# Two weights, then two stores: the order of transfers in one software queue of a batched matmul

## The chip, the cores and the metric

One core of a Trainium2 chip runs the kernel; the other cores are idle. PE is its tensor engine, DVE the vector engine, ACT the scalar engine; POOL and SP here mainly issue transfers, which 16 DMA engines carry out; PSUM is the memory that PE writes to. The metric is the device time of one execution in microseconds (us), as a median over repeated runs. A profile is one execution with the hardware profiler; its span runs from the first to the last instruction and is about 1.8 us shorter than the device time of the same run.

## The reference

```python
batch, m, k, n = 32, 512, 1024, 768
x      = randn(batch, m, k)   # float32
weight = randn(batch, k, n)   # float32
out    = matmul(x, weight)    # float32, batch by batch
```

It reads 67.1 MB of x and 100.7 MB of weights and writes 50.3 MB.

## The kernel before

Loads are issued from POOL, whose software queue casts float32 to bf16 on the way. Two batches of x come in one transfer (2 MiB at the destination), each weight in one (1.5 MiB at the destination, 3 MiB read), each output in one (1.5 MiB). PE transposes x through PSUM, then multiplies; ACT and DVE evict the result to `out_sb`. Four weight buffers, three of x, seven of the output. This is the loop's head, where the queue's order is made:

```python
AHEAD, LATE, HELD = 3, 4, 3
...
for b in range(B):                       # B = 32
    if b % 2 and b + AHEAD + 1 < B:
        ...                              # load the pair of x for batches b+4, b+5
    if b + AHEAD < B:
        load_w(b + AHEAD)                # waits until PE has used its buffer
    if b <= B - LATE:
        if b > 0:
            pending.append(b - 1)
        if b + AHEAD < B - HELD or b == B - LATE:
            for at in pending:
                nc.gpsimd.dma_start(out=out_view[at], in_=outs[at])
            pending = []
    ...                                  # transposes, matmuls, evictions of batch b
```

The last four weights are cut into two or three loads, and the last stores go through the SP queue.

## Time and profile before

| | before |
|---|---|
| median of the first 3 runs | 517.4 us (517.32 to 517.96) |
| span of the profiled run | 514.2 us |
| DMA busy | every slice of the span |
| PE busy | 85% |
| PE waits for a weight | 28.8 us in 10 waits |

The page splits the span into 40 slices and gives each engine's busy share in tenths. "DMA" is the mean of 16 DMA engines that work side by side on every transfer. A timeline line has start, duration, engine, source line, operation, tiles, and in brackets the idle time before it with what ended it. The lines themselves are in the prediction below.

### The profile page before, as it was taken

The page shows a single profiled execution, that of the slowest core. Times are in us where ns is not written, and L with a number is a line of the kernel's source. Part 1 is how long each engine was busy: PE and PEld are TensorE (multiplying, and loading weights), DVE is VectorE, ACT ScalarE, POOL GpSimd, SP SyncE. Part 2 cuts the span into 40 slices and gives each one's busy share as a digit, 9 for nine tenths or more (in the row PEclk, how much of TensorE's full clock was granted, in tenths as well). Part 3 has the DMA queues.
Part 4 walks back from the last instruction along what each step waited for, and adds up shares of the span by engine and source line. Part 5 has one row for each costly group of instructions (what it writes and reads, how often), then busy time and mean ns, then how long its engine had stood idle before and what let it go on. Part 6 is the DMA issues. An engine that isn't in the chain of part 4 may idle for free.

```text
span 514.2 us, 5846 instructions
## 1 busy us (share of the span) xinstructions
PE 438.1 (85%) x2576; PEld 279.6 (54%) x2576; DVE 130.0 (25%) x196; ACT 76.1 (15%) x129; POOL 43.8 (9%) x87
## 2 busy tenths in 40 slices
PE   2808999999999797998979889798897979999992
PEld 1506566666666463664636546365564645666561
DVE  1205142323223141231413205032050510514121
ACT  0100111111121111111111111011111111110211
POOL 3000100101010100101001000100001001011000
PEclk9957999999999898898989989799898997999997
DMA  8999999999999999999999999999999999999997
GB/s 240 224 220 214 221 265 289 214 278 273 272 287 213 282 270 276 279 215 293 263 277 275 221 292 250 278 278 224 305 239 277 277 235 306 224 276 214 270 428 318
DMA packets 12904, 135.63 MB, mean 264 GB/s; under 512 B 1488, under 2 KB 1488, under 8 KB 3280
## 3 DMA queue, kind: packets, MB, share of 16 engines
q0 software_dynamic: 11664, 126.88, 96.5%
q1 hardware_dynamic: 1216, 8.39, 4.1%
q8 instruction: 20, 0.33, 0.2%
q14 instruction: 4, 0.03, 0.0%
HBM read 167.77 MB, written 50.33 MB: 424 GB/s over the span
## 4 chain that ended last, share of the span: by engine, by line
PE 61%; DMA 25%; DVE 6%; another core or an unknown queue 4%; issue 1%; SPq 1%; ACT 0%
PE pm L121 54%; DMA w_sb<-in_weight_dram 18%; DMA out_sb<-in_x_dram 7%; PE pt L76 6%; DVE xT L83 4%; DVE out_sb L133 2%; SPq L143 1%; PE pt L103 0%; DVE xT L91 0%; ACT out_sb L134 0%; SPq L140 0%
## 5 line engine op out<-in xcount | busy, mean ns | idle before, releaser
L121 PE MATMUL pm<-w_sb,xT 128*128 128x256 bf16 (+1 forms) x2048 | 356.5, 338 | 28.8 <-DMA w_sb<-in_weight_dram 28.8
L121 PEld LDWEIGHTS <-xT 128*128 128x128 bf16 x2048 | 206.3, 101 | 174.6 <-DMA w_sb<-in_weight_dram 32.1
L133 DVE COPY out_sb<-pm 128x512 f32<-128x512 f32 x64 | 44.2, 691 | 331.8 <-PE pm L121 314.5
L76 PE MATMUL pt<-ident,x_sb 128*128 128x128 f32 x496 | 79.8, 302 | 10.5 <-DVE xT L83 10.2
L76 PEld LDWEIGHTS pt<-ident,x_sb 128*128 128x128 f32 x496 | 69.2, 209 | 21.5 <-DVE xT L83 18.7
L83 DVE COPY xT<-pt 128x1024 bf16<-128x1024 bf16 x120 | 77.4, 687 | 11.0 <-PE pt L76 11.0
L132 ACT COPY out_sb<-pm 128x512 f32<-128x512 f32 x64 | 37.4, 585 | 283.6 <-PE pm L121 276.0
L134 ACT COPY out_sb<-pm 128x512 f32<-128x512 f32 x64 | 37.5, 585 | 144.1 <-PE pm L121 144.0
L68 POOL DMA_DIRECT2D w_sb<-in_weight_dram x37 | 19.7, 533 | 328.7 <-PE pm L121 298.9
L167 POOL DMA_DIRECT2D out_dram<-out_sb x28 | 15.0, 536 | 60.3 <-DMA w_sb<-in_weight_dram 22.7
L103 PE MATMUL pt<-ident,out_sb 128*128 128x128 f32 x8 | 1.9, 421 | 16.2 <-DMA out_sb<-in_x_dram 16.2
L103 PE MATMUL pt<-ident,x_sb 128*128 128x128 f32 x24 | 5.2, 377 | 10.4 <-DMA x_sb<-in_x_dram 10.3
L104 DVE CAST xT<-pt 128x512 bf16<-128x512 f32 x8 | 5.9, 734 | 31.4 <-PE pt L103 31.1
L58 POOL DMA_DIRECT2D x_sb<-in_x_dram x15 | 8.0, 533 | 33.4 <-DMA out_dram<-out_sb 22.6
L103 PEld LDWEIGHTS pt<-ident,out_sb 128*128 128x128 f32 x8 | 1.6, 218 | 16.5 <-issue 16.5
L103 PEld LDWEIGHTS pt<-ident,x_sb 128*128 128x128 f32 x24 | 4.1, 210 | 11.3 <-issue 10.2
L91 DVE COPY xT<-pt 128x1024 bf16<-128x1024 bf16 x4 | 2.6, 686 | 0.2 <-PE pt L76 0.2
L132 ACT ACT_TABLE_LOAD x1 | 1.3, 1283 | 0.7 <-PEq L221 0.7
L62 POOL DMA_DIRECT2D x_sb<-in_x_dram x1 | 0.5, 527 | 6.7 <-DMA w_sb<-in_weight_dram 6.7
masks.py:199 POOL TENSOR_SCALAR_AFFINE_SELECT ident<-ident 128x128 f32<-128x128 f32 x1 | 0.3, 287 | 0.1
masks.py:197 POOL MEMSET ident<- 128x128 f32 x1 | 0.2, 223 | 0.0
L221 POOL MEMSET const-float32-0.0<- 128x1 f32 x1 | 0.1, 98 | 0.2 <-issue 0.2
(3 smaller groups left out, 0.3 us busy)
## 6 DMA issues: line engine op xcount, KB each, us to landing
w_sb<-in_weight_dram POOLq DMA_DIRECT2D x28, 1536.0 KB, 45.5
out_dram<-out_sb POOLq DMA_DIRECT2D x28, 1536.0 KB, 45.8
x_sb<-in_x_dram POOLq DMA_DIRECT2D x15, 2048.0 KB, 52.1
w_sb<-in_weight_dram POOLq DMA_DIRECT2D x7, 768.0 KB, 38.3
out_dram<-out_sb SPq DMA_DIRECT2D x4, 768.0 KB
out_dram<-out_sb SPq DMA_DIRECT2D x2, 1536.0 KB
x_sb<-in_x_dram SPq DMA_DIRECT2D x1, 1536.0 KB
x_sb<-in_x_dram POOLq DMA_DIRECT2D x1, 1024.0 KB, 36.2
```

The source lines that it names most:

```text
L58: nc.gpsimd.dma_start(out=xs[b], in_=pair_view[b // 2])
L68: nc.gpsimd.dma_start(out=ws[b][:, at:at + n, :], in_=w_view[b, :, at:at + n, :])
L76: nc.tensor.transpose(pt[:, j, :], pairs[:, mo, j::JT], ident)
L83: nc.vector.tensor_copy(both[:, :, :, :, half, :].rearrange("p b j i r -> p j b i r"), words(b, mt + MT * half).rearrange("p j (b i r) -> ...
L103: nc.tensor.transpose(pt[:, i, :], rows[:, JT * h + i::KT], ident)
L104: nc.vector.tensor_copy(xT[:, 2 * h:2 * h + 2].rearrange("p j m r -> p j r m"), pt.rearrange("p (j r) m -> p j r m", r=2),)
L121: nc.tensor.matmul(pm[bank][:, at:at + size], xT[:, ko // 2, :, ko % 2], ws[b][:, ko, off:off + size], start=(ko == 0 and not (together an ...
L132: nc.scalar.copy(o[:, 0:512], pm[0])
L133: nc.vector.tensor_copy(o[:, 512:1024], pm[1])
L134: nc.scalar.copy(o[:, 1024:N2], pm[2])
L143: nc.sync.dma_start(x_fourth[rows, 0], x_view[0, rows, MT - 1])
L167: nc.gpsimd.dma_start(out=out_view[at], in_=outs[at])
```

## The change

Its intent is to let loads follow loads and stores follow stores: in place of weight, store, weight, store, each pair of batches puts weight, weight, store, store into the software queue.

```diff
@@ -162,7 +162,7 @@
             if b <= B - LATE:
                 if b > 0:
                     pending.append(b - 1)
-                if b + AHEAD < B - HELD or b == B - LATE:
+                if b % 2 == 0 and b + AHEAD < B - HELD or b == B - LATE:
                     for at in pending:
                         nc.gpsimd.dma_start(out=out_view[at], in_=outs[at])
                     pending = []
```

A side effect at the end: the store of batch 24 moves behind the last weight.

## The prediction

> **What bounds the kernel now.** I read the page first for which engine is full, then the busy time by stage, then the waits of the tensor engine, then the issues of the software queue (POOL) in order of time, and last the end of the kernel.
>
> From the page (slices, queues, traffic):
>
> ```profile
> DMA  8999999999999999999999999999999999999997
> ...
> q0 software_dynamic: 11664, 126.88, 96.5%
> q1 hardware_dynamic: 1216, 8.39, 4.1%
> ...
> HBM read 167.77 MB, written 50.33 MB: 424 GB/s over the span
> ```
>
> The DMA engines are busy in every slice, and nearly all of it is the software queue, the one that the change reorders. The queue row counts bytes at the destination (loads are cast to bf16); the last line counts what crosses the memory interface, 218.1 MB in 514.2 us.
>
> Busy time by stage (columns: stretch, length, busy us and count of PE, PEld, DVE, ACT, POOL, then granted clock, DMA share, GB/s):
>
> ```profile
> 150.00:421.00 271.00, 240.00 (x1387) 151.30 (x1385) 69.98 (x107) 39.79 (x68) 22.83 (x43) 0.94 1.02 263
> 421.00:500.00 79.00, 73.60 (x442) 47.19 (x442) 20.38 (x31) 12.29 (x21) 5.82 (x11) 0.96 1.03 285
> ```
>
> From 150 to 421 us PE is idle for 31 us of 271 while the DMA share is 1.02 (packets overlap a little). Who makes PE wait there:
>
> ```profile
> PE pm L121 <- DMA w_sb<-in_weight_dram: 28.6, 9, 3.8
> PE pt L76 <- DVE xT L83: 6.1, 27, 0.3
> ```
>
> Nine waits of about 3.2 us, one per pair of batches. In the order of time (PE alone) each falls between the two batches of a pair:
>
> ```profile
> 283.62 10.56 PE L121 MATMUL pm<-w_sb,xT 128*128 128x512 bf16 x64
> 297.47 12.04 PE L121 MATMUL pm<-w_sb,xT 128*128 128x512 bf16 x64 [3.30 <-DMA w_sb<-in_weight_dram]
> 309.35 1.11 PE L76 MATMUL pt<-ident,x_sb 128*128 128x128 f32 x8
> ```
>
> The odd batch follows the transposes and finds its weight there; the even batch waits for its own, which comes right behind the 2 MiB load of x. The software queue in order of time:
>
> ```profile
> 168.11 0.53 POOL L68 DMA_DIRECT2D w_sb<-in_weight_dram  x1 [13.24 <-PE pm L121]
> 171.25 0.54 POOL L167 DMA_DIRECT2D out_dram<-out_sb  x1 [2.61 <-DMA w_sb<-in_weight_dram]
> 174.62 0.53 POOL L58 DMA_DIRECT2D x_sb<-in_x_dram  x1 [2.83 <-DMA out_dram<-out_sb]
> 183.25 0.53 POOL L68 DMA_DIRECT2D w_sb<-in_weight_dram  x1 [8.10 <-PE pm L121]
> 185.87 0.54 POOL L167 DMA_DIRECT2D out_dram<-out_sb  x1 [2.09 <-DVE xT L83]
> 199.31 0.53 POOL L68 DMA_DIRECT2D w_sb<-in_weight_dram  x1 [12.91 <-PE pm L121]
> 203.00 0.54 POOL L167 DMA_DIRECT2D out_dram<-out_sb  x1 [3.16 <-DMA w_sb<-in_weight_dram]
> 206.34 0.53 POOL L58 DMA_DIRECT2D x_sb<-in_x_dram  x1 [2.80 <-DMA out_dram<-out_sb]
> ```
>
> A weight is issued when PE frees its buffer; then a store or an x load may wait for an old transfer to land. Matching issues with landings, transfer i is never issued before transfer i-8 has landed: eight are in flight at most. By the view of one tile in windows that hold a single issue, the weight of 183.25 lands 51.0 us later, the store of 185.87 after 52.0, the weight of 199.31 after 45.8, the store of 203.00 after 45.8, the x load of 206.34 after 52.1. So the queue is some 50 us deep and PE lives on what was ordered long before.
>
> **What the Trainium skill says.** "HBM Reference", section Specifications: a core streaming alone measures about 425 GB/s, bounded by its 16 DMA engines. The page's 424 GB/s over the whole span, start and end included, agrees: there is no slack in the rate. "DMA: Bandwidth & Descriptors", section "Two DMAs through the same engine are not ordered": within one queue of an engine descriptors start in order. The landings above agree: they come in the order of issue. The same page, section "Anatomy of one DMA", says that the engines themselves do not wait on semaphores; waiting is done by the issuing sequencer. So reordering acts in two ways only: when POOL can issue, and which transfer is served first. Neither changes the bytes. I found no section that puts a price on alternating loads and stores in one queue, so the trace has to give it.
>
> **The change part by part.** No transfer, byte or arithmetic instruction is added or removed; the SP queue's issue list is the same. On POOL the pattern per pair, "x, even weight, store, odd weight, store", becomes "x, even weight, odd weight, store, store". At the end the store of batch 24, formerly between the weights of 28 and 29, moves behind the weight of 31, in front of the stores of 25 to 27.
>
> (1) Cost of a transfer by what precedes it. The spacing of landings is issue plus latency. Early: weight 46.18+29.2 = 75.4; store 47.00+32.0 = 79.0; weight 62.24+24.2 = 86.4; store 63.04+27.1 = 90.1; x 63.57+36.2 = 99.8; weight 72.64+34.4 = 107.0. So store after weight 3.6, weight after store 7.4, store 3.7, x after store 9.7, weight after x 7.2. The prologue has the case the change creates: weight 1 lands at 33.7, weight 2 directly behind it at 41.4, 7.7 apart; by the completion records of the earliest of the 16 engines it is 7.27, as for a weight after a store (7.27) and after x (7.28). Store after store occurs only at the end, 3.65 on the earliest engine. No switch shows a price over 0.1 us, and each of these spacings is its size over the same rate. Per pair: 9.7 + 7.3 + 3.65 + 7.3 + 3.65 = 31.6 us before, and the same five terms in another order after: 31.6. The steady period read off POOL, 389.95 minus 168.11 over seven pairs, is 31.7.
>
> (2) Arrival of weights. The even weight keeps its place behind x, so the 3.3 us wait of PE per pair stays. The odd weight comes one store earlier, 3.65 us. But it is not waited for: it lands at 199.31+45.8 = 245.1, and its batch can start its matmuls only after the even batch (which starts near 234 when its weight lands, and takes 12 us) and 6 us of transposes, so near 252. It had 7 us of slack and gets 11. Worth: 0.
>
> (3) The even store goes behind the odd weight in POOL's program, so it is issued about 16 us later (185.87 becomes about 200), and lands 7.3 us later. Its buffer is needed again seven batches on, about 110 us; in flight it was 52. Worth: 0.
>
> (4) Could the engines run dry? The queue is thinnest at 62.24 us: that weight lands after 24.2 us, of which 7.3 are its own and about 2 the completion, so some 15 us lie ahead of it. Without the store in front, 11 us. Still not dry, and later the backlog is 40 us and more. Worth: 0.
>
> (5) The end. The SP queue in order of time:
>
> ```profile
> 489.01 0.38 SPq L171 DMA_DIRECT2D out_dram<-out_sb  x1
> 489.44 1.75 SPq L173 DMA_DIRECT2D out_dram<-out_sb  x2
> 491.61 0.49 SPq L174 DMA_DIRECT2D out_dram<-out_sb  x1
> 503.31 1.63 SPq L205 DMA_DIRECT2D out_dram<-out_sb  x2
> ```
>
> Packets fill the 16 engines until about 509 us and the last lands near 512.6, while PE ends at 504.0. After its wait at 424.8 for the weight of batch 26, PE never again waits for a weight, so bringing weights 29 to 31 forward by 3.65 us doesn't make it end earlier. And the drain is what is left of the bytes: the store of 24 is one of them in either order. Worth: 0.
>
> The whole as a check: 32 weights x 7.3 = 234, 15 x pairs x 9.7 = 146, 32 stores x 3.65 = 117, the two single x loads 4.9 each, together 506 us of transfer time; the rest of 514 is the first issue, instruction fetches and the last completion. Sum of the change: 0 us. I predict 517.4.
>
> **The rivals.**
> - Fewer turns between reading and writing make the memory faster. Turns per pair halve, from two each way to one. For it: it is the likely intent. Against: the equal spacings in (1). At 0.1 us per turn and two turns in each of 12 pairs it would be 2.4 us, 515.0; a real gain of over 2% needs 10.4 us, 0.4 us per turn, which would be visible.
> - Holding back a store starves the queue, because POOL issues in order and now sits at the odd weight until PE frees its buffer, with at most eight in flight. If a whole store's time were lost per pair, 12 x 3.65 = 44 us, 561. Against: 11 us of backlog at the thinnest point and DMA share 1.02.
> - The odd weight's earlier arrival feeds PE. If PE were the bound, up to 3.3 us per pair, some 30 us. Against: the wait is for the other weight, and the DMA total would still forbid it.
> - The end shifts by a store: 3.65 us better if the last weight set it (513.7), as much worse if the moved store hung over alone (521.1). Against: full engines on both sides of the last matmul. A partial effect of 1 us is what I allow for.
>
> **Range and chances.** Center 517.4. The three runs spread by 0.6, small end effects and small turn costs are worth about 1 us either way, so 516.3 to 518.6 for 8 in 10. Faster by over 2% has 1.5%, slower by over 2% has 1.5% (a stall I have overlooked in POOL's order), within 2% has 97%.
>
> **What would show it right or wrong.** Right: DMA full in every slice, 31.6 to 31.7 us per pair, PE still waiting about nine times for the even weight for some 29 us, PE ending near 504, the stores' median time to landing shorter, because half of them are issued later. Step 1 is wrong if the pair's period changes; step 2 if PE's waits move or go; step 3 if an eviction waits for a store; step 4 if the DMA share falls under 1 anywhere between 46 and 160 us; step 5 if the period holds and the span moves.

## More of the kernel before

One detail of the start turns out to matter: the fourth block of the first x (128 rows of 4 KB) comes in 14 loads, 12 of them of five rows each.

```python
few = [slice(at, first + 20, 4) for first in (0, 20, 40) for at in range(first, first + 4)]
for rows in (slice(64, P), slice(60, 64), *few):
    nc.sync.dma_start(x_fourth[rows, 0], x_view[0, rows, MT - 1])
```

## The result, and the profile after

A ratio here is the mean time of one kernel's fast runs over that of the other's fast runs of the same rounds, so it is not quite the ratio of the medians quoted.

| | before | changed |
|---|---|---|
| median of 6 runs each | 517.36 us (515.72 to 518.04) | 515.04 us (514.86 to 515.37) |
| ratio, 95% interval | | 0.9961, 0.9943 to 0.9979 |
| span of the profiled run | 514.2 us | 513.6 us |

The change is faster by 0.4%, 2 us, outside the range of the prediction; the interval excludes no change. Two things stand out before any profile is read. The changed kernel's runs lie within 0.5 us, those of the kernel before are spread over 2.3 us. And the profiled run of the kernel before was one of its shorter ones (515.96 us), so its two traces differ by 0.6 us where the medians differ by 2.3.

The page of the changed kernel, the same rows as before:

```profile
DMA  8999999999999999999999999999999999999997
...
q0 software_dynamic: 11664, 126.88, 96.5%
q1 hardware_dynamic: 1216, 8.39, 4.1%
...
HBM read 167.77 MB, written 50.33 MB: 425 GB/s over the span
```

In these rows only the rate tells the two apart, 425 GB/s in place of 424: the same packets and bytes, DMA full in every slice. The busy time by stage of the changed kernel:

```profile
150.00:421.00 271.00, 239.33 (x1379) 150.84 (x1378) 69.88 (x106) 39.80 (x68) 22.38 (x42) 0.93 1.02 264
421.00:500.00 79.00, 73.92 (x459) 47.73 (x458) 20.48 (x31) 12.35 (x22) 6.35 (x12) 1.00 1.02 286
```

PE still has 32 us of idle time in the first stretch and still spends it on the even weight, as the order of time on PE shows (changed kernel, one pair):

```profile
283.07 10.56 PE L121 MATMUL pm<-w_sb,xT 128*128 128x512 bf16 x64
297.22 13.16 PE L121 MATMUL pm<-w_sb,xT 128*128 128x512 bf16 x64 [3.59 <-DMA w_sb<-in_weight_dram]
310.22 1.12 PE L76 MATMUL pt<-ident,x_sb 128*128 128x128 f32 x8
```

The software queue of the changed kernel in order of time, one pair:

```profile
184.29 0.53 POOL L68 DMA_DIRECT2D w_sb<-in_weight_dram  x1 [5.40 <-PE pm L121]
200.36 0.53 POOL L68 DMA_DIRECT2D w_sb<-in_weight_dram  x1 [15.54 <-PE pm L121]
200.93 0.54 POOL L167 DMA_DIRECT2D out_dram<-out_sb  x1
202.92 0.54 POOL L167 DMA_DIRECT2D out_dram<-out_sb  x1 [1.45 <-DMA w_sb<-in_weight_dram]
209.90 0.53 POOL L58 DMA_DIRECT2D x_sb<-in_x_dram  x1 [6.45 <-DMA w_sb<-in_weight_dram]
```

This is as foreseen: POOL sits 15.5 us at the odd weight, the even store leaves with the odd one, and the limit of eight in flight now holds up the x load.

So where is the time? A transfer has no row of its own on the page, but the view of one tile in a window that holds a single issue gives the time from issue to landing. For the x load of the last pair (batches 29 and 30), kernel before:

```profile
L58 POOL DMA_DIRECT2D x_sb<-in_x_dram x1: 528/528/528, 396.8 to 396.8; - x1
...
DMA to landing us min/median/max: 52.2/52.2/52.2
```

Changed kernel:

```profile
L58 POOL DMA_DIRECT2D x_sb<-in_x_dram x1: 532/532/532, 399.9 to 399.9; - x1
...
DMA to landing us min/median/max: 48.2/48.2/48.2
```

It lands at 396.8+52.2 = 449.0 us before and at 399.9+48.2 = 448.1 us after. From there to the end of the span it is 65.2 us before and 65.5 us after. The x load of batches 5 and 6, read the same way, lands at 68.1 and 68.2. So the 12 pairs between the two landings took 380.9 us before and 379.9 after: the difference is in the steady part, is in the transfers themselves, and is small and spread out.

The trace's record of single packets, below the views, says what kind of time it is. A weight is 128 packets, eight per DMA engine, and nearly all take 0.926 us. Some are longer. I counted weight packets over 0.946 us after the first 20 us, leaving out those that overlap in time with one of the 16 KB instruction fetches that use the same engines:

```text
                      longer packets   time above 0.926 us, summed over the 16 engines
kernel before         96               16.2 us
changed kernel        29                4.5 us
```

And I sorted the weight packets between 60 and 445 us by what other engines did at their midpoint:

```text
                                    kernel before              changed kernel
a store is beginning elsewhere      538, of which 68 longer    227, of which 13 longer
a store is ending elsewhere         265, of which  0 longer      0
no store elsewhere                 1930, of which 28 longer   2564, of which 16 longer
```

The 16 engines work through the same list, but not in step: the first is 2.4 us ahead of the last by 50 us (spread of the 16 completions of the second x pair). When the leading engines have started on a store, the lagging ones still read the last packets of the weight ahead of it, and most of the stretched packets are among those: 68 of 96 before, 13 of 29 in the changed kernel. The traces place the rest too: of those with no store elsewhere, 25 of 28 and all 16 have their midpoint in the last 1 us before the first packet of a store. So nearly all stretched packets lie at a turn from weight to store, but not on lagging engines alone. With pairs, half as many weights stand directly ahead of a store.

Is the stretch enough for the time? Divided by 16 it is 1.0 us per engine before and 0.3 in the changed kernel. The mean over the 16 completions, from the second x pair to the weight of batch 28, took 405.3 and 404.7 us. Four runs told of below, e1, e4, h1 and h2, have 1.2, 1.4, 0.0 and 0.0 us of stretch per engine and took 405.7, 405.9, 404.3 and 404.4. So the stretch accounts for the differences in the steady part to within 0.3 us.

### The profile page after: what moved, and what is told of

It reads as the page before. It is cut to its first block, busy times and chain, and to the rows that moved or that the text cites. A ratio compares the mean times of both kernels' runs of the same rounds, so it can differ in the third digit from the quotient of the medians.

```text
span 513.6 us, 5846 instructions
## 1 busy us (share of the span) xinstructions
PE 436.0 (85%) x2576; PEld 279.1 (54%) x2576; DVE 130.0 (25%) x196; ACT 76.2 (15%) x129; POOL 44.0 (9%) x87
## 4 chain that ended last, share of the span: by engine, by line
PE 39%; DMA 35%; issue 16%; DVE 4%; another core or an unknown queue 3%; POOL 1%; ACT 0%; POOLq 0%
PE pm L121 35%; DMA w_sb<-in_weight_dram 27%; DMA out_dram<-out_sb 6%; PE pt L76 4%; DVE xT L83 2%; DMA x_sb<-in_x_dram 2%; DVE out_sb L133 1%; POOL w_sb L68 0%; POOL x_sb L58 0%; POOL out_dram L167 0%; DVE xT L91 0%; ACT out_sb L134 0%; POOLq L167 0%; POOLq L68 0%
```

## The experiments

Three theories went in, and were put in numbers before each run (two more, an issue and a contention theory, stand in some expectations). **Turns:** each change from weight to store has a fixed price. **End:** the store of batch 24 behind the last weight gives the gain. **Luck:** the times of the kernel before fall into groups by chance, and the order has nothing to do with it. The **lag theory** came after the first seven: the stretch depends on how far the engines are apart.

| run | order of the queue | median us (range) | ratio to before, 95% interval |
|---|---|---|---|
| e1_before_again | before, unchanged | 517.59 (515.79 to 517.7) | 1.0008, 0.9981 to 1.0035 |
| e2_after_again | changed, unchanged | 515.09 (514.78 to 515.62) | 0.9966, 0.9944 to 0.9989 |
| e3_pairs_only | pairs, end as before | 514.96 (514.89 to 515.14) | 0.9964, 0.9942 to 0.9986 |
| e4_end_only | end changed, pairs as before | 516.42 (515.55 to 517.79) | 0.9995, 0.997 to 1.002 |
| e5_fours | four stores in a row | 515.73 (515.64 to 515.75) | 0.9996, 0.9983 to 1.0008 |
| e6_halves_adjacent | before, transfers halved | 517.63 (517.5 to 518.44) | 1.0036, 1.0023 to 1.0049 |
| e7_halves_alternating | halves alternate | 517.62 (517.55 to 517.79) | 1.0034, 1.002 to 1.0047 |
| d1_dma_alternating | transfers alone, before | 516.69 (516.37 to 516.87) | 1.0002, 0.9982 to 1.0023 |
| d2_dma_pairs | transfers alone, pairs | 517.61 (516.98 to 517.76) | 1.0018, 0.9995 to 1.004 |
| d3_dma_stores_last | transfers alone, stores last | 515.76 (515.58 to 516.04) | 0.9985, 0.9965 to 1.0006 |
| g1_alternating_even_start | before, even start | 516.1 (516.06 to 517.27) | 0.9997, 0.998 to 1.0015 |
| g2_pairs_even_start | changed, even start | 517.0 (516.88 to 517.61) | 1.0014, 0.9997 to 1.0031 |
| h1_alternating_more_lag | before, more lag | 515.22 (515.16 to 515.32) | 0.9976, 0.996 to 0.9992 |
| h2_pairs_more_lag | changed, more lag | 515.79 (515.76 to 516.21) | 0.9989, 0.9972 to 1.0005 |
| i1_alternating_half_lag | before, half of that lag | 517.08 (515.46 to 518.3) | 1.0015, 0.9996 to 1.0034 |
| h3_more_lag_again | as h1 | 515.24 (515.16 to 515.29) | 0.9984, 0.9971 to 0.9997 |
| e9_after_third | changed, unchanged | 515.14 (515.04 to 515.61) | 0.9984, 0.997 to 0.9999 |
| e8_x_between | weight, weight, x, store, store | 515.2 (514.88 to 515.49) | 0.9983, 0.997 to 0.9996 |

Each set of runs was made on one chip, the five sets on chips 1, 11, 3, 8 and 9. Runs e1 to e4 shared one set of 11 runs of the kernel before (median 517.15), e5 to e7 one of 9 (515.96), d1 to d3 one of 11 (516.45), g1 to h2 one of 11 (516.54), and the last four one of 11 (515.87). Because the kernel before moves that much between sets, the medians of one set are compared with each other first.

### Is the gain real, and which part of the change makes it?

Control, the kernel before with no edit:

> The kernel before, unchanged, as a control of the noise and for a second profile of it. All theories: ratio 1.000 to the kernel before, within 0.2%. Runs between 515.7 and 518.0 us, as the six so far lay (two near 515.8, four near 517.6). Turn theory (each change from weight to store in the queue slows the weight packets of the engines that lag behind): some 130 weight packets over 0.946 us in the trace, clustered where the first engines begin a store; if this profile is one of the longer runs, it has more of that excess than the 20 us (summed over the engines) of the first profile. Luck theory (the two groups of times are a state of the chip): the excess is the same in short and long runs.

The changed kernel with no edit:

> The changed kernel, unchanged, to measure the gain again on another day and chip. Turn theory and end theory: 0.9955 to 0.997 of the kernel before, 514.8 to 515.4 us, runs within 0.6 us of each other. Luck theory: the ratio comes back to 0.999 to 1.001.

The pairs alone:

```diff
-                if b + AHEAD < B - HELD or b == B - LATE:
+                if b % 2 == 0 and b + AHEAD < B - HELD or b in (B - LATE - 3, B - LATE):
```

> The pairing of the twelve pairs alone: the store of batch 24 stays where it was, between the weights of 28 and 29. Turn theory: nearly the whole gain, ratio 0.996 to 0.9972, 515 to 515.9 us, and about half as many stretched weight packets as before. End theory (the gain comes from the store of batch 24 that moved behind the last weight): ratio 0.999 to 1.001, 517 us.

The end alone:

```diff
-                if b + AHEAD < B - HELD or b == B - LATE:
+                if b + AHEAD < B - HELD - 1 or b == B - LATE:
```

> The end alone: the kernel before with the store of batch 24 behind the last weight, the pairs as they were. Turn theory: one turn of 25 less, ratio 0.9992 to 1.0002, 517.0 to 517.5 us. End theory: the whole gain, 0.9955 to 0.997, 515 us. In both the weights of batches 29 to 31 land about 3.65 us earlier.

Measured: the gain repeats (0.9966), and the pairs alone have all of it (0.9964). The end alone has none that can be told from noise (0.9995, interval 0.997 to 1.002). The end theory falls. The kernel before, run again, spread over 1.9 us, and the copies beside it over 4 us (514.93 to 518.91), while both kernels with pairs stayed within 0.9 us. Luck as a state of the chip falls too, since runs of both orders took turns on the same chip.

The run of the end alone gave by chance the profile of a long run, 515.8 us, in the order of the kernel before. Its x load of the last pair:

```profile
L58 POOL DMA_DIRECT2D x_sb<-in_x_dram x1: 528/528/528, 399.2 to 399.2; - x1
...
DMA to landing us min/median/max: 51.8/51.8/51.8
```

It lands at 451.0 us, 2.0 us later than in the short run of the kernel before, and from there to the end it takes 64.8 us, no longer than the others. Its stretched weight packets, counted as above, number 130 with 21.6 us in excess. The second profile of the unchanged kernel, e1, has 57 with 19.2 us, 18.2 of it between 128 and 192 us: single packets took up to 2.09 us there. So the length of a run of the old order is made in the same place as the gain of the new one, and can come in a burst.

### Does a turn have a fixed price?

If 12 turns fewer are worth 2 us, fewer still should be worth more. Stores in groups of four:

```diff
-                if b + AHEAD < B - HELD or b == B - LATE:
+                if b % 4 == 0 and b + AHEAD < B - HELD or b == B - LATE:
```

> Stores in groups of four behind every second pair: six turns from weight to store where the kernel before has 24 and the changed one 12. Turn theory with a fixed price per turn (2.1 us for 12 turns, 0.17 us each): one more us, ratio 0.994 to 0.9955, 513.5 to 514.3 us, and the stretch of weight packets at half of the changed kernel's 8 us (summed over engines). Turn theory in which the long runs of the kernel before come from a lag that feeds on itself: the feeding is already gone with pairs, so 0 to 0.5 us more, 514.5 to 515.1 us. Issue theory (the gain comes from POOL issuing the odd weight earlier, whatever the switches): no further gain or a loss, 515 us or more.

More turns: every transfer of a weight or an output in halves, first adjacent as a control, then alternating (cut to its core; the store loop then issues the second half only):

```diff
-        for n in CHUNKED.get(b, (KT,)):
+        for n in CHUNKED.get(b, (4, 4)):
             nc.gpsimd.dma_start(out=ws[b][:, at:at + n, :], in_=w_view[b, :, at:at + n, :])
             at += n
+            if between is not None and at < KT:
+                half = slice(0, N2)
+                nc.gpsimd.dma_start(out=out_view[between, :, half], in_=outs[between][:, half])
```

> A control for the next run: every weight and every store in two halves that follow each other, so the switches are those of the kernel before (24) and only the number of transfers grows. Turn theory: 516.5 to 518.5 us, ratio 0.998 to 1.003, unless eight half transfers in flight are too few, which would show as a DMA share below 1.

> The same halves as in the run before it, but weight half, store half, weight half, store half: about 50 turns from weight to store in place of 24, the same transfers otherwise. Turn theory: slower than the control with adjacent halves by 2 to 6 us (0.4 to 1.2%), with more weight packets stretched. Issue theory: the same as the control within 0.5 us.

Both answers go against a fixed price. Groups of four took 515.73 us, which is no better than the pairs' 515.0 to 515.1 in other sets (and on other chips), with fewer stretched packets (8, 1.4 us). Twice as many turns cost nothing against the control (517.62 against 517.63), although halving itself costs 1.7 us. The alternating halves even had fewer stretched packets (7, 0.4 us) than the adjacent ones (61, 6.3 us); their 12 pairs took 381.8 us against 382.4, but the gain did not last to the end. My expectation of 2 to 6 us was plainly wrong. The issue theory (the gain comes from POOL issuing the odd weight earlier) had both answers right, so these two runs don't exclude it. Against it stand the DMA share, 1.02 with either order, and a run further below, h1: the old order, without the earlier issue, in 515.2 us.

Then the disputed cost by itself: the same loads and stores without any transposes, matmuls or evictions. The stores write zeros, so the result is wrong.

```diff
-    ... transposes, matmuls, evictions ...
+        zero = out_pool.tile([P, MT * N], F32, name="out_sb")
+        nc.vector.memset(zero, 0.0)
+        def store(at):
+            nc.gpsimd.dma_start(out=out_view[at], in_=zero)
...
+            if FLUSH:        # d1: True; d2: b % 2 == 0 or b == B; d3: b == B
+                for at in pending:
+                    store(at)
+                pending = []
```

> The loads and stores alone, wrong result on purpose (zeros are stored; no transposes, matmuls or evictions): weight, store, weight, store as in the kernel before. Turn theory, if the price is in the DMA engines and the memory alone: about 508 to 512 us, 1.5 to 3 us longer than the next run. Contention theory (the weight packets are stretched because compute engines use the on-chip memory at that moment): the same as the next run within 0.4 us, and few stretched packets.

> The same transfers alone, in the changed order: weight, weight, store, store. Turn theory: 1.5 to 3 us shorter than the run before it, 506 to 509 us. Contention theory: the same within 0.4 us.

> The same transfers alone, all loads first and all stores at the end: one turn. Turn theory with a fixed price: shorter than the pairs by the price of 15 turns, about 2 us. Turn theory with a self-feeding lag: shorter by 0 to 1 us. Contention theory: the same as the two before it within 0.4 us.

The transfers alone take as long as the whole kernel, which confirms what bounds it. But here the pairs are slower than alternating, by 0.9 us, where every version of the turn theory had them faster. One turn in place of many gained another 0.9 us on alternating. Neither the turn theory nor contention with the compute engines explains that sign. The stretch does go with it: 33 stretched weight packets (9.3 us) alternating, 52 (12.4 us) with pairs, none with the stores last. So stretching needs no compute and no instruction fetch, and where no store runs among the loads there is none. Of the 33, 22 lie in the 2.5 us before the first store of the run.

### Does the lag between the engines decide?

The transfers alone differ from the kernel in more than the compute: the first x is one load, the last four weights are whole, the last stores stay in POOL's queue, and all stores read one buffer. Two differences show in the traces. In the kernel the 16 completions of the second x pair are spread over 2.4 us, with five engines 2.0 to 2.4 us behind; in the transfers alone the spread is 0.7 us (0.8 with pairs). And the kernel fetches its instructions through the DMA engines, 20 packets of 16 KB that take 0.89 to 0.98 us each. The five late engines are explained by the start. The page "DMA: Bandwidth & Descriptors" in the Trainium skill, section "Why a DMA increments its semaphore by 16 and not by 1", says that a transfer uses the largest number of engines up to 16 that divides its slowest dimension; five rows then go to five engines. The trace agrees: 60 of those packets, 4 KB each and 0.172 us long, are 12 per engine, 12 x 0.172 = 2.1 us, and the five were seen 2.0 to 2.4 us behind.

So I took the lag away, and added to it, in both orders. Even start:

```diff
-        for rows in (slice(64, P), slice(60, 64), *few):
+        for rows in (slice(0, P),):
```

> The order of the kernel before, with the fourth block of the first x loaded by one transfer over all 16 engines in place of 14 small ones, 12 of which put their bytes on five engines only. Lag theory: the spread between the first and the last of the 16 completions of the second x pair falls from 2.4 to under 1 us, weight packets are stretched less, and the gap to the next run (pairs) is under 1 us. Fixed price per turn: the gap to the next run stays at 2 us.

> The changed order with the same even start. Lag theory: within 1 us of the run before it, both near 514 to 516 us (the slowest engine is then one of those that also fetch instructions). Fixed price per turn: 2 us shorter than the run before it.

More lag on the same five engines, by rows that nobody reads:

```diff
+        scratch = const.tile([P, N], F32)
+        for rows in few[:8]:
+            nc.sync.dma_start(scratch[rows], x_view[0, rows, 0, :N])
```

> The order of the kernel before with 8 more small loads at the start (rows nobody reads), about 1 us more on the same five engines. Lag theory: 1 us for the bytes, plus more stretch: 518 to 520 us, and the gap to the next run is 2.5 us or more. Fixed price per turn: 1 us longer than the kernel before, gap 2 us.

> The changed order with the same 8 small loads. Lag theory: 515.5 to 517 us, 2.5 us or more shorter than the run before it. Fixed price per turn: 516 us, 2 us shorter.

| spread after the second x pair | alternating | pairs |
|---|---|---|
| 1.8 and 2.0 us (even start; 1.2 and 1.6 one load later) | 516.1 us | 517.0 us |
| 2.4 us (as in the kernel) | 516.5 us, from 514.9 to 517.9 | 515.04 to 515.14 us in three other sets, on other chips |
| 3.3 and 3.2 us (more lag) | 515.2 us | 515.8 us |

The start decides which order is ahead, though not as I had expected. I had foreseen that more lag widens the gap in favour of pairs. Instead pairs win only at the kernel's own start; at both others alternating is ahead, by 0.9 and 0.6 us. The two gaps are not of one kind. With the even start the 12 pairs, measured as above, took 382.3 us alternating and 383.3 with pairs. With more lag they took 379.7 us in both, and the 0.6 us fell after the landing of the last x pair: 64.7 us to the end alternating, 65.2 with pairs. So more lag leaves no difference between the orders in the steady part. And with more lag the old order ran in a band of 0.2 us, with 2 stretched weight packets (0.3 us) where the kernel before had 96. With pairs and more lag there was none. The pairs with an even start had 63 (12.1 us), with the order that was to avoid them, and alternating had 21 (5.8 us).

The even start is no gain in itself: in the changed kernel's trace, followed engine by engine (the record does not name a packet's engine, so packets were joined end to end), most of the other eleven engines lose 2.2 to 2.7 us to 450 us, and the five late ones 0.8 to 1.7. I put the larger losses down to the instruction fetches; if so, the odd little loads at the start balance the fetches on the other engines. No run separates the two, so this is not shown.

The last set repeats this on one chip, at half the dose, and tries another order:

```diff
+        for rows in few[:4]:          # i1, in place of few[:8]
```

> The order of the kernel before with 4 small loads more at the start, half the dose: the spread after the second x pair is near 2.9 us, between 2.4 (kernel before) and 3.3 (8 loads). Lag theory (stretching only while the lag is some 1 to 3 us): if the limit lies under 2.9, 514.9 to 515.4 us in a narrow band and under 5 us of stretch in the weight packets; if above, 515 to 518 us as the kernel before. Fixed price per turn: as the kernel before plus 0.5 us.

> The order of the kernel before with 8 small loads more, again, now beside the changed kernel. Lag theory: 515.0 to 515.5 us in a band of 0.5 us, within 0.3 us of the changed kernel of the same call. Luck: back to 516 to 518 us.

> The changed kernel on the same chip as the two runs before it: 514.8 to 515.5 us, as in both earlier sets.

For the order weight, weight, x, store, store, the load of the next pair of x is issued at the even batch behind its weight and ahead of the two stores:

```diff
-            if b % 2 and b + AHEAD + 1 < B:        # x ahead of the even weight
-                ...
             if b + AHEAD < B:
                 load_w(b + AHEAD)
+            if b % 2 == 0 and 0 < b and b + AHEAD + 2 < B:
+                ...                                # x of the next pair, behind the odd weight
```

> The changed order with the load of x moved between the two weights and the two stores: weight, weight, x, store, store, so that no weight is directly ahead of a store. Lag theory with any load affected: x packets are stretched instead of weight packets, 515 to 516 us. If only weights ahead of stores are affected: neither is stretched, 514.0 to 515.0 us. Fixed price per turn, whatever the load: as the changed kernel, 515.0.

The old order with more lag repeated at 515.24 us in a band of 0.13 us, beside the changed kernel at 515.14. Its x load of the last pair:

```profile
L58 POOL DMA_DIRECT2D x_sb<-in_x_dram x1: 527/527/527, 396.9 to 396.9; - x1
...
DMA to landing us min/median/max: 51.8/51.8/51.8
```

It lands at 448.7 us, 0.3 us ahead of the kernel before, although the x load of the first steady pair lands 0.9 us later (69.0 against 68.1): the 12 pairs took 379.6 us against 380.9. Half the dose, a spread of 2.9 us, left the old order as wide as ever, 515.46 to 518.3, with 44 stretched packets (6.2 us) in the profile of its shortest run. Taken by these starts, the stretching stops between 2.9 and 3.2 us of lag (3.2 in the repeat, with 9 stretched packets and 1.0 us); a store keeps one engine busy for 3.65 us. With x between, the x packets ahead of the stores were stretched (20 of them, 3.8 us) and hardly a weight packet (3, 1.1 us): any load there is affected, not weights alone. Its time is that of the changed kernel.

No version beats the changed kernel clearly. The pairs with the end as before (514.96), the old order with more lag (515.2) and x between (515.2) all reach the same 515 us.

## Why the prediction was right or wrong

- **What bounds the kernel** was right. The transfers alone take 515.8 to 517.6 us.
- **Step 1, no price for a switch,** failed, and is the cause of the miss. It read the spacing of completions in the first 110 us, partly on the earliest of the 16 engines, and a resolution of 0.1 us per switch leaves room for 2.4 us in 24. The price is paid mostly after 128 us (7 of the 96 stretched packets come before 110 us), on early engines as well as late ones: over the 12 pairs the first of the 16 completions took 380.6 us before and 379.9 after, the last 380.9 and 379.9. So the period per pair fell by 0.08 us where step 1 had it unchanged. There the spacing is not the size over the rate: 96 weight packets were stretched in the short profile of the kernel before, 130 in a long one, against 29 in the changed kernel. What came in its place is not the fixed price of the first rival either. That rival's 0.1 us per turn gave 515.0 by luck: fewer turns gained nothing more, more turns cost nothing, and with other starts the gain in the steady part was gone or turned.
- **Step 2** was right: PE waits for a weight 10 times for 29.0 us in all, 28.8 before.
- **Step 3** was right: no eviction is listed as waiting for a store.
- **Step 4** was right: the DMA share of the changed kernel is 1.00 to 1.03 in four stretches from 46 to 160 us and 1.02 after them, and no run dry is seen. Its 15 us ahead of the thinnest weight had a completion time taken off that no trace shows; without it 24.2 - 7.3 = 16.9 us lie ahead, and 13 us without the store.
- **Step 5** was right in its sum: from the last x pair's landing to the end it is 65.2 us before and 65.5 after, and the end alone moved nothing. A detail was wrong: PE begins its last batch at 491.4 us in place of 493.4, for the even weight came earlier and the clock from 421 to 500 us was 1.00 in place of 0.96. It doesn't matter, because the stores behind it set the end.
- **The range** failed on its own. It took the 0.6 us between three runs for the kernel's noise. Over the 59 runs of the kernel before that served for comparison (e1's six left out), its median is 516.3 us and its range 514.8 to 518.9; the changed kernel's 18 runs go from 514.8 to 515.6. The three runs that I had were from the slower part. The change hardly alters the best run; it takes away the slow ones. The means of these runs, 516.4 and 515.1 us, differ by 0.25%, less than the first comparison's 0.4%.

What is shown is that the pairs make the gain (e3), that it arises in the steady part, and that packets stretched at turns account for it there. Open is why the stretching starts and stops with the lag: what the lagging reads and the leading writes share is in no record of these traces. That the stretch adds to the lag until the lag exceeds a store's 3.65 us and then stops fits e1 (spread 2.9 us before the burst, 4.5 after it and hardly a stretched packet), the runs with more lag (4.0 us) and the half dose, which had 2 of its 44 stretched packets from 128 to 208 us, at a spread of 3.4 to 3.5 us, and 30 from 320 us on, at 3.1 us and less. It does not fit the long run e4, where the spread went from 4.0 to 4.9 us and packets went on being stretched. So the spread as one number is not the whole of it; which engines lag must count too. Also open is why pairs cost 0.9 us in the steady part with the even start, and 0.6 us in the end with more lag; the end alone varies by as much between runs of one kernel (65.2 and 64.7 us in two profiles of the kernel before).

## What to carry to other kernels

With all DMA engines full, the slowest of the 16 set the end here: its landing of the last x pair plus 64.5 to 65.5 us was the span in every run of the kernel that kept x ahead of the weights, and the 2.4 us that five engines lost at the start stayed. So look at the spread of its completions and not only at the mean or the first. An order of loads and stores that is faster may owe it to how far the engines happen to be apart, so test it again after any change to the start of the kernel. A change that narrows the spread of the times shows only in the ratio of many runs: three runs of the old kernel said 517.4, its shortest are no slower than the new one.

## What the Trainium skill lacked or had wrong

- "DMA: Bandwidth & Descriptors", section "Two DMAs through the same engine are not ordered", says that nothing orders DMAs across the 16 engines, but not how far they drift or what it costs. Here they were 2.4 us apart by 50 us and 2.4 to 3.1 us apart until 460 us, up to 5.1 us in another run of the same kernel, with all of them busy.
- The same page has no price for alternating loads and stores in one queue. Here it lies between none (2 stretched packets with more lag) and 2 us of 515 (the kernel's own start), and it falls on load packets beside the start of a store or in the 1 us before it: 0.926 us became up to 2.09 us.
- The same page gives the number of engines that a transfer uses, which held (five rows, five engines), but not that such a transfer leaves those engines behind for the rest of a DMA-bound kernel: 12 loads of 20 KB, 2.1 us.
- "Runtime: NRT & Kernel Launch", section "Instruction fetch mechanics", has instructions fetched in 16 KiB blocks through a DMA queue, but not what that takes from DMA engines that are all busy. Here 20 packets of 16 KB took 0.89 to 0.98 us each.
